# RWKV layers of a six-layer kernel: gate columns on four column groups, R projections in the chunk loop, the bonus term formed earlier, and the two halves of the heads five steps apart

## The chip, the cores and the metric

The kernel runs on one core of one Trainium2 chip. The metric is the time of one execution on the device in microseconds, as the median of several runs. The engines are named as in the profile: PE (TensorE, matrix products), DVE (VectorE), ACT (ScalarE), POOL (GpSimd) and SP (SyncE, which issues DMA transfers). PE runs at one of two levels, 1.2 or 2.4 GHz; the profile gives the granted clock as a share of the full one, so 0.50 is 1.2 GHz.

## What is computed

The model has width 1024, sequence length 256 and 16 heads of 64. It has six layers; two of them (the first, and the fourth) mix over time by RWKV-7, the others by attention, and four have a feed-forward part. The change touches the RWKV mixing only:

```python
r, k, v = rkv[:, :, 0], rkv[:, :, 1], rkv[:, :, 2]      # 1024 x 1024 projections
logw = -softplus(-(w0 + tanh(xw @ w1) @ w2)) - 0.5;  decay = exp(-exp(logw))
a = sigmoid(a0 + (xa @ a1) @ a2)
g = sigmoid(xg @ g1) @ g2                               # the gate, inner width 160
kk = heads(k * k_k), normalised;  k = k * (1 + (a - 1) * k_a)
def step(state, inp):
    sa = einsum('bhvk,bhk->bhv', state, kk_t)
    state = state * w_t - sa[..., None] * (kk_t * a_t) + v_t[..., None] * k_t
    return state, einsum('bhvk,bhk->bhv', state, r_t)
y = group_norm(y) * ln_w + ln_b
y = y + sum(r * k * r_k, axis=-1, keepdims=True) * v    # the bonus term
out = (y * g) @ w_out
```

## The kernel before

**How the step-by-step recurrence is computed.** The 256 steps are two chunks of 128. Within a chunk the recurrence is a triangular linear system for each of the 16 heads, so 32 systems of 128 x 128 unknowns are solved by matrix products. Features lie on the 128 partitions in eight feature chunks c = 0 to 7, two heads in each.

**The stages of one layer.** First come the token mixes, the value projection and the small low-rank products (`lora1` is the first factor of the gate: its inner width of 160 is 128 columns and 32 more, summed over eight slices k of the input). Then the *chunk loop* over c: `kproj` is the key projection, `prep` scales the key vectors by the decay, `amat` forms the products of a system on PE, and `wmat` its right-hand side. `rproj(c)` projects R for a feature chunk, 24 matmuls in split fp32r (lines L117 to L119) plus an elementwise product Rh on DVE; two of the eight are in this loop, six come later.

The *inverse chain* (`inv_diag`) inverts the 32 x 32 diagonal blocks: copies into D by DVE and ACT, a transpose, and 62 dependent DVE operations (L1330 and L1332). While it runs, PE does the remaining R projections and, for every c, `rmat(c)` (products of R with K, L1225) and `rout(c)` (bo, the bonus coefficients, L1237; and the products with V, L1243). rmat's result leaves PSUM by four ACT copies and two POOL masks (L919); the product `prod` on DVE (L1228) has two buffers, freed by bo.

The *merge* (`inv_merge`) puts the inverse together from 32 to 64 to 128: first products L1360, second L1374 and L1376, third L1384, fourth L1387. At four places in it `turn()` calls `gtc`, the gate's second factor, for two feature chunks at a time: a matmul with 128 rows and one with 32 rows for each, into one bank, and a copy to GT (L1266 to L1268).

The *tail* (`rwkv_tail`) is written as a generator with eight steps for each half q of the heads: corrected values (L1425, L1452), state (L1460), outputs (L1435, L1468, L1485), bonus term (L1476, L1478), group norm, transposes (L1498), the gated result z (L1502) and its split og. The two halves A and B run two steps apart; leftover `rout` and `gtc` calls are drawn in by `need`, `need_gate` and `fill`. The output projection (`ohalf`) takes og of each half.

**What sets the order.** The program is written in this order, and a scheduler then decides the order on each engine, with buffers from pools as constraints. Each engine works its own queue strictly in order.

## Time and profile before

| | |
|---|---|
| runs | 1863.23, 1864.0, 1868.2 us (median 1864.0) |
| profiled execution | own time 1852.14 us, span 1850.4 us |
| busy share of the span | PE 95%, DVE 74%, ACT 55%, POOL 2% |
| granted PE clock, mean | 0.952 |
| chain of work that ended last | PE 73%, DVE 14%, DMA 5%, ACT 3%, issue 2% |

The two RWKV layers lie at 0 to 273 us and at about 1085 to 1360 us of the span. A busy share is an average over stages with different limits, and a busy PE at clock 0.50 does half the work; so each stage is read from its own window, with its clock.

### The profile page before, as it was taken

The page shows a single profiled execution, that of the slowest core. Times are in us where ns is not written, and L with a number is a line of the kernel's source. Part 1 is how long each engine was busy: PE and PEld are TensorE (multiplying, and loading weights), DVE is VectorE, ACT ScalarE, POOL GpSimd, SP SyncE. Part 2 cuts the span into 40 slices and gives each one's busy share as a digit, 9 for nine tenths or more (in the row PEclk, how much of TensorE's full clock was granted, in tenths as well). Part 3 has the DMA queues.
Part 4 walks back from the last instruction along what each step waited for, and adds up shares of the span by engine and source line. Part 5 has one row for each costly group of instructions (what it writes and reads, how often), then busy time and mean ns, then how long its engine had stood idle before and what let it go on. Part 6 is the DMA issues. An engine that isn't in the chain of part 4 may idle for free.

```text
span 1850.4 us, 34035 instructions
## 1 busy us (share of the span) xinstructions
PE 1756.0 (95%) x13699; PEld 1575.6 (85%) x13699; DVE 1375.6 (74%) x2710; ACT 1013.8 (55%) x1832; POOL 40.5 (2%) x78
## 2 busy tenths in 40 slices
PE   7998989999999999999999989999899998997998
PEld 5677789999899999877999966787899997885876
DVE  8869489866688876799887568686787656676665
ACT  4755345545576455567645445754265445664664
POOL 0003000000000000000000000021000000000000
PEclk9989789999999999999999999886899999998999
DMA  5211138746427855632685542211065455432540
GB/s 214 103 52 55 59 113 323 259 157 228 168 93 279 288 183 172 237 137 92 239 295 191 182 164 102 73 57 47 35 223 188 170 192 193 160 137 91 181 159 23
DMA packets 52841, 292.19 MB, mean 158 GB/s; under 512 B 6611, under 2 KB 9435, under 8 KB 27980
## 3 DMA queue, kind: packets, MB, share of 16 engines
q1 hardware_dynamic: 48540, 284.64, 43.4%
q10 hardware_dynamic: 4144, 5.39, 0.9%
q8 instruction: 107, 1.75, 0.4%
q14 instruction: 50, 0.41, 0.1%
HBM read 287.90 MB, written 2.10 MB: 157 GB/s over the span
## 4 chain that ended last, share of the span: by engine, by line
PE 73%; DVE 14%; DMA 5%; ACT 3%; issue 2%; DVEq 0%; ACTq 0%
PE mm L117 14%; PE mm L118 14%; PE mm L119 14%; PE mm L222 5%; PE mm L223 5%; PE mm L224 5%; DMA adaw<-ada 4%; DVE wlo L111 3%; DVE junk L678 2%; PE o L511 1%; PE at L475 1%; PE mm L1184 1%; PE at L1165 1%; PE mm L1266 1%; PE mm L1267 1%
## 5 line engine op out<-in xcount | busy, mean ns | idle before, releaser
L111 DVE TENSOR_TENSOR wlo<-wraw,whi 128x1024 fp32r<-128x1024 f32 (+2 forms) x518 | 588.3, 1140 | 229.5 <-ACT whi L110 227.3
L110 ACT CAST whi<-wraw 128x1024 fp32r<-128x1024 f32 (+2 forms) x518 | 504.2, 982 | 296.9 <-PE mm L119 174.3
L222 PE MATMUL mm<-whi,xgh 128*128 128x512 f32 x192 | 80.9, 421 | 8.5 <-ACT xgh L737 8.5
L1549 ACT ACTIVATE sg<-gt 128x256 f32<-128x256 f32 x88 | 36.7, 417 | 90.0 <-DVE gt L1546 89.8
L117 PE MATMUL mm<-mh,whi 128*128 128x256 f32 x256 | 80.9, 316 | 5.0 <-DVE Rh L1097 3.8
L118 PE MATMUL mm<-mh,wlo 128*128 128x256 f32 x256 | 77.9, 304 | 0.0
L119 PE MATMUL mm<-ml,whi 128*128 128x256 f32 x256 | 77.8, 304 | 0.0
L223 PE MATMUL mm<-wlo,xgh 128*128 128x512 f32 x192 | 77.2, 402 | 0.0
L224 PE MATMUL mm<-whi,xgl 128*128 128x512 f32 x192 | 77.0, 402 | 0.0
L678 DVE SCALAR_TENSOR_TENSOR junk<-adaw,cs 128x1024 f32<-128x1024 f32 x48 | 58.6, 1221 | 17.9 <-DMA adaw<-ada 17.7
L1546 DVE TENSOR_TENSOR gt<-mm,rr 128x512 f32<-128x512 f32 x88 | 60.5, 687 | 8.5 <-PE mm L119 5.7
L117 PEld LDWEIGHTS mm<-mh,whi 128*128 128x128 f32 x256 | 55.2, 216 | 9.0 <-DVE Rh L1097 4.0
L118 PE MATMUL mm<-xg0h,wlo 128*128 128x256 f32 x192 | 53.8, 280 | 5.2 <-DVE wlo L111 5.1
L118 PEld LDWEIGHTS mm<-mh,wlo 128*128 128x128 f32 x256 | 55.2, 216 | 1.7 <-issue 1.7
L119 PEld LDWEIGHTS mm<-ml,whi 128*128 128x128 f32 x256 | 54.7, 214 | 1.7 <-issue 1.7
L117 PE MATMUL mm<-xg0h,whi 128*128 128x256 f32 x192 | 54.6, 284 | 0.0
L119 PE MATMUL mm<-xg7l,whi 128*128 128x256 f32 x192 | 53.2, 277 | 0.6 <-DVE xg7l L135 0.6
L222 PEld LDWEIGHTS mm<-whi,xgh 128*128 128x128 f32 x192 | 37.4, 195 | 18.9 <-ACT xgh L737 9.4
L117 PE MATMUL mm<-xg4h,whi 128*128 128x256 f32 x192 | 53.5, 278 | 0.0
L117 PE MATMUL mm<-xg7h,whi 128*128 128x256 f32 x192 | 53.2, 277 | 0.0
L119 PE MATMUL mm<-xg0l,whi 128*128 128x256 f32 x192 | 53.1, 277 | 0.0
L117 PE MATMUL mm<-xg1h,whi 128*128 128x256 f32 x192 | 53.1, 277 | 0.0
(831 smaller groups left out, 6067.1 us busy)
## 6 DMA issues: line engine op xcount, KB each, us to landing
wraw<-ffn_gu SPq DMA_DIRECT2D x88, 1024.0 KB, 6.1
wraw<-ffn_dn SPq DMA_DIRECT2D x64, 704.0 KB, 4.0
adaw<-ada SPq DMA_DIRECT2D x48, 512.0 KB, 5.7
wraw<-hy_qkv SPq DMA_DIRECT2D x24, 1024.0 KB, 4.9
wraw<-rw_k SPq DMA_DIRECT2D x8, 1024.0 KB, 4.9
wraw<-rw_r SPq DMA_DIRECT2D x8, 1024.0 KB, 4.9
wraw<-rw_out SPq DMA_DIRECT2D x8, 1024.0 KB, 4.8
wraw<-sb_qk SPq DMA_DIRECT2D x8, 1024.0 KB, 4.8
```

The lines of the kernel that those rows point to most:

```text
L110: nc.scalar.copy(hi, rw)
L111: nc.vector.tensor_tensor(out=lo, in0=rw, in1=hi.bitcast(F32), op=ALU.subtract)
L117: mm(ps, w[0], x[0], start=first, stop=False, **kw)
L118: mm(ps, w[1], x[0], start=False, stop=False, **kw)
L119: mm(ps, w[0], x[1], start=False, stop=last, **kw)
L222: mm(ps, x[0], w[0], start=first, stop=False)
L223: mm(ps, x[0], w[1], start=False, stop=False)
L224: mm(ps, x[1], w[0], start=False, stop=last)
L475: nc.tensor.matmul(z[e][:, o:o + n], qT[b, hp, t * 128:t * 128 + 128], kT[b, hp, :n], start=True, stop=True)
L678: nc.vector.scalar_tensor_tensor(out=junk, in0=raw, scalar=1.0, in1=self.cs, op0=ALU.mult, op1=ALU.mult, accum_out=self.mod[l][:, j:j + 1])
L1546: nc.vector.tensor_tensor(out=gt, in0=ps.rearrange("p (a b) -> p a b", a=2), in1=r[:, None, :].to_broadcast([128, 2, S]), op=ALU.mult)
L1549: nc.scalar.activation(sg, gt[:, 0], AF.Silu)
```

## The change

The gate's inner 32 columns are computed four times, on the four column groups of PE, so that sg2 lies on all 128 partitions; the gate's second factor then takes four matmuls of 128 rows and four of 32 rows on four row groups into four banks, twice instead of four times, once among the rmat and rout calls and once at the merge's first turn. All eight R projections stand in the chunk loop (RPC says how many at each c). All rmat and rout calls come before the merge. The bonus term bv is formed ahead of the merge, in its own buffer, in place of the eight operations of the tail. The tail has no draw-ins; half A runs alone for five steps, and the projection of its result is laid into half B's steps, two pieces at a time. The weights of the gate's second factor are laid out anew on the host for this, before the launch.

```diff
 BIG = 1e30
 WCH = 2048
-RPC = (3, 6)
-RPN = len(RPC)
-RFR = (0, 0, 2, 2, 2, 2, 3, 3)
-RLAG, RFA, RFB, RFO = 2, 0, 0, 2
+RPC = (0, 0, 1, 1, 1, 1, 2, 2)
+RLAG, RFO = 5, 2
...
-GTP = {}
...
-            sg2 = sp.tile([32, S], F32, name="sg2")
+            sg2 = sp.tile([128, S], F32, name="sg2")
...
-                    for k in range(KT):
-                        t = mix(m, k, "xg_", 8)
+                    for k in range(0, KT, 4):
+                        xt_ = [(k + j, mix(m, k + j, "xg_", 8)) for j in range(4)]
                         for q in range(0, n, 128):
                             p = min(128, n - q)
-                            mm(ps[:p, q // 128 * S:q // 128 * S + S], w[:, o + k * stride + q:o + k * stride + q + p], t,
-                               start=(k == 0 and q == 0), stop=(k == KT - 1), skip_group_check=True)
+                            for k1, t in xt_:
+                                for g in range(0, 128, p):
+                                    mm(ps[g:g + p, q // 128 * S:q // 128 * S + S], w[:, o + k1 * stride + q:o + k1 * stride + q + p], t,
+                                       start=(k1 == 0 and q == 0), stop=(k1 == KT - 1), skip_group_check=True)
                     return ps
...
-                act(sg2, ps[:32, S:], AF.Sigmoid)
+                act(sg2, ps[:, S:], AF.Sigmoid)
...
-                rp = iter(range(RPN))
+                rp = iter(range(KT))
...
                             rnorm(1)
-                    elif c in RPC:
+                    for _ in range(RPC[c]):
                         rproj(rb, next(rp))
                     wmat(c)
                 x2p.close()
                 act(scol, scol, AF.Exp)
+            self.xctx.close()
             with ExitStack() as rde:
                 rd = rde.enter_context(tc.tile_pool(name="rd", bufs=1))
                 TT = [rd.tile([128, 16, 128], F32, name="TT0")]
                 nc.gpsimd.memset(TT[0], 0.0)
                 X = self.inv_diag(rd, AKB)
-                re = rde.enter_context(tc.tile_pool(name="re", bufs=2))
+                rt = rde.enter_context(tc.tile_pool(name="rt", bufs=1, side="right"))
+                GT = rt.tile([128, KT, S], F32, name="GT")
+                TT.append(rt.tile([128, 16, 128], F32, name="TT1"))
+                act(TT[1], self.ones[:, None, :128].to_broadcast([128, 16, 128]), AF.Copy, scale=0.0)
+                g2 = self.wraw.tile([128, WCH], F32, name="wraw")
+                nc.sync.dma_start(g2[:, :1024], self.a["rw_g2a"][l])
+                nc.sync.dma_start(g2[:, 1024:1280], self.a["rw_g2b"][l])
+
+                def gtc(a):
+
+                    pg = [self.psum("at")[:, :S] for _ in range(4)]
+                    for j in range(4):
+                        c = 4 * a + j
+                        mm(pg[j], g2[:, c * 128:128 + c * 128], sg1, start=True, stop=False)
+                    for j in range(4):
+                        b = slice(32 * j, 32 * j + 32)
+                        mm(pg[j], g2[b, 1024 + a * 128:1152 + a * 128], sg2[b], start=False, stop=True)
+                    for j in range(4):
+                        cp(GT[:, 4 * a + j], pg[j])
+                rex = ExitStack()
...
+                re = rex.enter_context(tc.tile_pool(name="re", bufs=2))
                 bo = self.psum("o")
                 ark = [re.tile([128, 4, 128], F32, name=f"ark{j}", bufs=1) for j in range(2)]
                 prods = {}
@@ -1248,62 +1268,39 @@
...
                                               for c in range(KT)), [])
-                for c in range(RPN, KT):
-                    rproj(re, c)
-                    for _ in range(RFR[c]):
-                        rph.pop(0)()
-                self.xctx.close()
-                rt = rde.enter_context(tc.tile_pool(name="rt", bufs=1, side="right"))
-                GT = rt.tile([128, KT, S], F32, name="GT")
-                g2 = self.wraw.tile([128, WCH], F32, name="wraw")
-                nc.sync.dma_start(g2[:, :1024], self.a["rw_g2a"][l])
-                nc.sync.dma_start(g2[:32, 1024:], self.a["rw_g2b"][l])
-
-                def gtc(c0):
-                    pg = self.psum("mm")
-                    for c in (c0, c0 + 1):
-                        o = (c - c0) * S
-                        mm(pg[:, o:o + S], g2[:, c * 128:128 + c * 128], sg1, start=True, stop=False)
-                        mm(pg[:, o:o + S], g2[:32, 1024 + c * 128:1152 + c * 128], sg2, start=False, stop=True)
-                    cp(GT[:, c0:c0 + 2], pg.rearrange("p (a b) -> p a b", a=2))
-                TT.append(rt.tile([128, 16, 128], F32, name="TT1"))
-                act(TT[1], self.ones[:, None, :128].to_broadcast([128, 16, 128]), AF.Copy, scale=0.0)
+                for j, f in enumerate(rph):
...
+                    f()
+                    if j == 8:
+                        gtc(0)
+                rex.close()
+                bv = rde.enter_context(tc.tile_pool(name="rv", bufs=1)).tile([128, 2, 4, 2, 2, 64], F32, name="bv")
+                for q in range(2):
+                    for ch in range(2):
+                        bc = lambda u: u[:, ch, 8 * q:8 * q + 8].rearrange("p (c e) -> p c e", e=2)[:, :, :, None].to_broadcast([128, 4, 2, 64])
+                        tt(out=bv[:, q, :, ch], in0=Vc[:, ch, 512 * q:512 * q + 512].rearrange("p (c e v) -> p c e v", e=2, v=64),
...
                 XNT = self.inv_turn(rd, X)
-                og, gts = [None] * KT, [lambda c=c: gtc(c) for c in range(0, KT, 2)]
-
+                og, gts = [None] * KT, [lambda: gtc(1)]
                 sc = [scr[:, 1024 * q:1024 * q + 1024] for q in range(2)]
-                self.inv_merge([u.rearrange("p a h t -> p (a h) t") for u in AKB], XNT, TT, sc, lambda: gts.pop(0)())
+                self.inv_merge([u.rearrange("p a h t -> p (a h) t") for u in AKB], XNT, TT, sc, lambda: gts and gts.pop()())
...
-                                          sc[q], C, og, lambda: [rph.pop(0)() for _ in range(max(0, len(rph) - 8 * (1 - q)))],
-                                          lambda: [gts.pop(0)() for _ in range(max(0, len(gts) - 2 * (1 - q)))])
+                    return self.rwkv_tail(q, rc, rt, l, Vc, AKB[q], KB, TT[q], csT, Rh, N0, W00, WK1, scol, bv[:, q], GT, sc[q], C, og)
                 add = lambda c, ps: self.new_x(c, x[c], ps)
-                fills = [rph, gts, []]
-
-                def fill(n):
-                    for _ in range(n):
-                        for f in fills:
-                            if f:
-                                f.pop(0)()
-                                break
-                A, B, i = chain(0), chain(1), 0
+                A, B, i, rest = chain(0), chain(1), 0, []
                 while A or B:
-                    if A:
-                        if next(A, 1):
-                            A = None
-                            fills[2] = self.ohalf(self.a["rw_out"][l], 0, og, add)
-                        fill(RFA)
-                    if B and i >= RLAG:
-                        if next(B, 1):
-                            B = None
-                        fill(RFB if A else RFO)
-                    for _ in range(GTP.get(i, 0)):
-                        if gts:
-                            gts.pop(0)()
+                    if A and next(A, 1):
+                        A = None
+                        rest = self.ohalf(self.a["rw_out"][l], 0, og, add)
+                    if B and i >= RLAG and next(B, 1):
+                        B = None
+                    for f in rest[:RFO]:
+                        f()
+                    rest = rest[RFO:]
                     i += 1
-                for f in fills[2] + self.ohalf(self.a["rw_out"][l], 1, og, add):
+                for f in rest + self.ohalf(self.a["rw_out"][l], 1, og, add):
                     f()
             return x
 
@@ -1404,7 +1401,7 @@
...
-        need()
...
                 mm(ps[:, j], TT[:, 8 + 4 * g + j], W1[:, 4 * g + j], start=True, stop=True)
-            (nc.vector.tensor_copy if g else cp)(UP[:, 4 * g:4 * g + 4], ps)
+            cp(UP[:, 4 * g:4 * g + 4], ps)
...
         tt(out=o, in0=y_group(1, lambda j: UP[:, j, :64]), in1=o, op=ALU.add)
         yield
-        bv = TT.rearrange("p h t -> p (h t)")[:, :1024].rearrange("p (c a e v) -> p c a e v", c=4, a=2, e=2)
-        for ch in range(2):
-            bc = lambda u: u[:, ch, hq].rearrange("p (c e) -> p c e", e=2)[:, :, :, None].to_broadcast([128, 4, 2, 64])
-            tt(out=bv[:, :, ch], in0=Vc[:, ch, 512 * q:512 * q + 512].rearrange("p (c e v) -> p c e v", e=2, v=64),
-                                    in1=bc(mu), op=ALU.add)
-            tt(out=bv[:, :, ch], in0=bv[:, :, ch], in1=bc(coef), op=ALU.mult)
         norm(0)
         yield
...
-        need_gate()
...
-    out["rw_g2a"], out["rw_g2b"] = np.ascontiguousarray(f("rw_g2")[:, :128]), np.ascontiguousarray(f("rw_g2")[:, 128:])
+    out["rw_g2a"] = np.ascontiguousarray(f("rw_g2")[:, :128])
+    out["rw_g2b"] = np.ascontiguousarray(f("rw_g2")[:, 128:].reshape(2, 32, 2, 4, 128).transpose(0, 3, 1, 2, 4).reshape(2, 128, 256))
     out["rw_v2"] = np.concatenate([f("rw_v2")[0], f("rw_v0")], 0)
     rk = np.zeros((2, 128, 8, 2), np.float32)
```

PE, between the chunk loop and the merge of the first RWKV layer. Before, a piece of the chain's time, where R projections (mm<-mh,whi and its two partners, 24 matmuls for each) stand between rout (L1237, L1243) and rmat (L1225):

```order
L119 MATMUL mm<-ml,whi 128x256
L1237 MATMUL o<-rkb,prod 128x2 x2
L1243 MATMUL mm<-Vc,ark_1475 128x64 x4
L1225 MATMUL at<-Rh,KB 128x128 x8
L1237 MATMUL o<-rkb,prod 128x2 x2
L1243 MATMUL mm<-Vc,ark_1474 128x64 x4
L117 MATMUL mm<-mh,whi 128x256
L118 MATMUL mm<-mh,wlo 128x256
```

Of the change, from the last W product on (L1245 is rmat, L1257 is bo, L1263 the products of rout):

```order
L1183 MATMUL mm<-Vc,akk_665 128x64 x4
L1245 MATMUL at<-Rh,KB 128x128 x16
L1257 MATMUL o<-rkb,prod 128x2 x6
L1245 MATMUL at<-Rh,KB 128x128 x2
L1263 MATMUL mm<-Vc,ark_1712 128x64 x4
L1245 MATMUL at<-Rh,KB 128x128 x6
L1263 MATMUL mm<-Vc,ark_1713 128x64 x4
L1245 MATMUL at<-Rh,KB 128x128 x8
L1263 MATMUL mm<-Vc,ark_1712 128x64 x4
L1245 MATMUL at<-Rh,KB 128x128 x8
L1257 MATMUL o<-rkb,prod 128x2 x2
```

The projections are gone from between them: rmat and rout follow each other directly, and six bo matmuls (three chunks) stand ahead of the third rmat.

DVE, in the last third of the inverse chain of the same layer (X and tmp are the chain's own tiles). Before:

```order
L1228 TENSOR_TENSOR prod<-Rh,KB 128x256 [waits PE_49]
L1332 TENSOR_TENSOR X__1404<-X__1404,tmp__1407 128x9x23 [waits DVE_49]
L1330 TENSOR_TENSOR tmp__1407<-A__1402,X__1404 128x192 [waits DVE_49]
L1332 TENSOR_TENSOR X__1404<-X__1404,tmp__1407 128x8x24 [waits DVE_49]
L1330 TENSOR_TENSOR tmp__1407<-A__1402,X__1404 128x175 [waits DVE_49]
L1332 TENSOR_TENSOR X__1404<-X__1404,tmp__1407 128x7x25 [waits DVE_49]
L1330 TENSOR_TENSOR tmp__1407<-A__1402,X__1404 128x156 [waits DVE_49]
L111 TENSOR_TENSOR wlo<-wraw,whi 128x1024 [waits DMAHW1_49,Activation_49]
L1332 TENSOR_TENSOR X__1404<-X__1404,tmp__1407 128x6x26 [waits DVE_49]
L1097 TENSOR_TENSOR Rh<-mm,E1r 128x256 [waits PE_49]
```

Of the change, the same place:

```order
L1327 TENSOR_TENSOR tmp__1636<-A__1631,X__1633 128x207 [waits DVE_49]
L1329 TENSOR_TENSOR X__1633<-X__1633,tmp__1636 128x9x23 [waits DVE_49]
L1280 TENSOR_TENSOR bv<-Vc,mu 128x4x128 [waits PE_49,Pool_49]
L1327 TENSOR_TENSOR tmp__1636<-A__1631,X__1633 128x192 [waits DVE_49]
L1282 TENSOR_TENSOR bv<-bv,coef 128x4x128 [waits DVE_49]
L1329 TENSOR_TENSOR X__1633<-X__1633,tmp__1636 128x8x24 [waits DVE_49]
L1280 TENSOR_TENSOR bv<-Vc,mu 128x4x128
L1327 TENSOR_TENSOR tmp__1636<-A__1631,X__1633 128x175 [waits DVE_49]
L1282 TENSOR_TENSOR bv<-bv,coef 128x4x128 [waits DVE_49]
L1329 TENSOR_TENSOR X__1633<-X__1633,tmp__1636 128x7x25 [waits DVE_49]
```

The products of prod, the weight halves (wlo) and Rh have left this place, and the bonus term's operations (L1280, L1282) stand between those of the chain; the first of them waits for PE and POOL.

PE, at the start of the merge (sg and wraw are the gate's inner values and its weights; XN and AKB the merge's first product). Before:

```order
L1225 MATMUL at<-Rh,KB 128x128 x8
L1237 MATMUL o<-rkb,prod 128x2 x4
L1360 MATMUL mm<-XN__1883,AKB_625 32x32 x32
L1360 MATMUL mm<-XN__1883,AKB_626 32x32 x32
L1266 MATMUL mm<-sg_112,wraw 128x256
L1267 MATMUL mm<-sg_113,wraw 128x256
L1266 MATMUL mm<-sg_112,wraw 128x256
L1267 MATMUL mm<-sg_113,wraw 128x256
L1374 MATMUL mm<-M_1887,XT__1885 32x32
L1376 MATMUL at<-XT__1885,M_1887 32x32 x2
```

Of the change:

```order
L1257 MATMUL o<-rkb,prod 128x2 x2
L1226 MATMUL at<-sg_112,wraw 128x256 x2
L1263 MATMUL mm<-Vc,ark_1713 128x64 x4
L1226 MATMUL at<-sg_112,wraw 128x256 x2
L1229 MATMUL at<-sg_113,wraw 128x256 x4
L1357 MATMUL mm<-XN__1953,AKB_649 32x32 x32
L1357 MATMUL mm<-XN__1953,AKB_650 32x32 x32
L1371 MATMUL mm<-M_1957,XT__1955 32x32 x16
L1373 MATMUL at<-XT__1955,M_1957 32x32 x32
```

The gate's second product now stands around the last rout, ahead of the merge's first product, and none stands inside the merge.

## Rows read from the trace of the kernel before

**Rows 1.** Windows: span, engines' busy us (instructions), granted PE clock, DMA share, GB/s.
```profile
97.00:138.40 41.40, 38.04 (x280) 32.69 (x278) 29.85 (x76) 21.36 (x63) 1.03 (x2) 0.84 0.09 31
...
144.90:183.50 38.60, 30.80 (x278) 28.85 (x276) 37.02 (x81) 19.47 (x53) 13.12 (x16) 0.92 0.16 56
183.50:216.70 33.20, 33.15 (x480) 23.65 (x480) 10.35 (x15) 14.55 (x21) 0.00 (x0) 0.57 0.15 46
216.70:247.40 30.70, 25.08 (x284) 23.43 (x283) 24.33 (x55) 7.68 (x20) 0.00 (x0) 0.92 0.10 39
247.40:273.30 25.90, 25.90 (x201) 25.80 (x200) 21.69 (x49) 14.94 (x28) 0.00 (x0) 0.90 0.43 164
...
1269.20:1302.20 33.00, 32.98 (x480) 23.50 (x480) 10.37 (x15) 14.53 (x21) 0.00 (x0) 0.59 0.14 45
```

**Rows 2.** Timeline of PE in an R projection: start, us, instruction.
```profile
143.40 0.28 PE L117 MATMUL mm<-mh,whi 128*128 128x256 f32 x1
...
145.75 0.28 PE L119 MATMUL mm<-ml,whi 128*128 128x256 f32 x1
```

**Rows 3.** Timeline of ACT; in brackets idle time before, and its releaser.
```profile
138.87 4.50 ACT L1319 COPY D__1393<-AKB 32x512 f32<-32x512 f32 x4
...
144.34 0.64 ACT L1231 COPY ark<-at 128x256 f32<-128x256 f32 x2
...
175.33 1.91 ACT L1270 ACTIVATE TT<-ones 128x2048 f32<-128x2048 f32 x1 [2.15 <-PE mm L119]
...
200.84 0.59 ACT L1268 COPY GT<-mm 128x512 f32<-128x512 f32 x1 [4.04 <-PE mm L1267]
```

**Rows 4.** Timeline of DVE, chain and half B's last og.
```profile
143.40 1.25 DVE L1322 STREAM_TRANSPOSE A__1402<-D__1393 128x1024 f32<-128x1024 f32 x1
...
144.98 1.21 DVE L111 TENSOR_TENSOR wlo<-wraw,whi 128x1024 fp32r<-128x1024 f32 x1
...
181.55 1.91 DVE L1338 STREAM_TRANSPOSE XN__1883<-X__1404 128x1024 f32<-128x1024 f32 x1
...
258.13 0.43 DVE L1504 TENSOR_TENSOR og<-z,og 128x256 fp32r<-128x256 f32 x1
```

**Rows 5.** Timeline of PE in the chunk loop, half clock and full.
```profile
123.62 1.22 PE L1165 MATMUL at<-aT,KB 64*128 64x128 f32 x8 [1.93 <-DVE KB L1155]
...
127.88 1.23 PE L1165 MATMUL at<-aT,KB 64*128 64x128 f32 x8
...
134.12 1.00 PE L1184 MATMUL mm<-Vc,akk 128*128 128x64 f32 x8
135.06 1.16 PE L1165 MATMUL at<-aT,KB 64*128 64x128 f32 x16
```

**Rows 6.** Windows in the merge, columns as in rows 1.
```profile
204.00:208.00 4.00, 4.00 (x11) 1.93 (x10) 0.00 (x0) 0.58 (x1) 0.00 (x0) 0.50 0.00 0
...
212.00:216.00 4.00, 4.00 (x40) 2.61 (x37) 0.80 (x2) 1.17 (x2) 0.00 (x0) 1.00 0.41 98
```

**Rows 7.** Timeline of PE, merge and tail.
```profile
205.48 1.22 PE L1267 MATMUL mm<-sg,wraw 32*128 32x256 f32 x2
...
214.70 2.08 PE L1387 MATMUL at<-TT,aT 64*64 64x64 f32 x32
...
225.08 2.00 PE L1243 MATMUL mm<-Vc,ark 128*128 128x64 f32 x16
```

**Rows 8.** Groups by line and shape: line, operation, shapes, count, busy us, mean ns.
```profile
L1008 PE MATMUL mm<-xm,G 128*128 128x256 f32 x16 | 5.5, 424 | 0.0
L1008 PE MATMUL mm<-xm,G 128*32 128x256 f32 x16 | 5.0, 391 | 0.0
...
L1452 PE MATMUL at<-WK,TT 128*128 128x128 f32 x32 | 4.2, 280 | 0.0
...
L1468 PE MATMUL at<-KB,AKB 128*64 128x128 f32 x32 | 2.2, 279 | 0.0
...
L1476 DVE TENSOR_TENSOR TT<-Vc,mu 128x512 f32<-128x512 f32 x4 | 2.7, 688 | 2.0 <-PE mm L1425 2.0
```

More of the change, by code (lines that the diff above doesn't have):

```diff
@@ L1269, in rwkv @@
-                TT.append(rt.tile([128, 16, 128], F32, name="TT1"))
-                act(TT[1], self.ones[:, None, :128].to_broadcast([128, 16, 128]), AF.Copy, scale=0.0)
+                for j, f in enumerate(rph):
[8 more added lines that the diff above has]
+                        tt(out=bv[:, q, :, ch], in0=Vc[:, ch, 512 * q:512 * q + 512].rearrange("p (c e v) -> p c e v", e=2, v=64),
+                           in1=bc(mu), op=ALU.add)
+                        tt(out=bv[:, q, :, ch], in0=bv[:, q, :, ch], in1=bc(coef), op=ALU.mult)
@@ L1278, in chain @@
                 def chain(q):
-                    return self.rwkv_tail(q, rc, rt, l, mu, Vc, AKB[q], KB, TT[q], csT, Rh, N0, W00, WK1, scol, coef, GT,
-                                          sc[q], C, og, lambda: [rph.pop(0)() for _ in range(max(0, len(rph) - 8 * (1 - q)))],
-                                          lambda: [gts.pop(0)() for _ in range(max(0, len(gts) - 2 * (1 - q)))])
+                    return self.rwkv_tail(q, rc, rt, l, Vc, AKB[q], KB, TT[q], csT, Rh, N0, W00, WK1, scol, bv[:, q], GT, sc[q], C, og)
@@ L1405, in inv_merge, with rwkv_tail @@
                 turn()
-    def rwkv_tail(self, q, rc, rt, l, mu, Vc, AKB, KB, TT, csT, Rh, N0, W00, WK1, scol, coef, GT, scr, C, og, need, need_gate):
+    def rwkv_tail(self, q, rc, rt, l, Vc, AKB, KB, TT, csT, Rh, N0, W00, WK1, scol, bv, GT, scr, C, og):
         nc = self.nc
```

## The prediction

> **What bounds the kernel now.** I read the busy shares of the page first, to see that no engine is full everywhere, then the timeline of one RWKV layer engine by engine, then windows cut at its stage borders, and last the granted clock in those windows, because the same work of TensorE (PE) costs twice as much at the lower of its two levels (0.5 of 2.4 GHz, that is 1.2 GHz). The change touches only the two RWKV layers; they read alike (the merge takes 33 us and a clock of 0.57 to 0.59 in both), so I work out one and count it twice [rows 1].
>
> The reader is to see five stages with different limits. In the chunk loop (97 to 138.4) PE is busy 38 of 41 us, part of it at half clock. In the inverse chain (144.9 to 183.5) VectorE (DVE) is busy 37 of 38.6 us: it runs 62 dependent small operations, one stream, and everything else that it is given lies in the middle of them. In the merge (183.5 to 216.7) PE is busy throughout, but at a clock of 0.57. The tail of the heads (216.7 to 247.4) shares its time between PE and DVE, and the output projection up to the next layer's first matmul (247.4 to 273.3) is PE again [rows 1].
>
> **The change, part by part.**
>
> *The R projections.* One costs 24 matmuls; 20 steps take 2.35 us at full clock, so 2.82 us each [rows 2]. Six move from the chain's time into the chunk loop, 16.9 us. The loop's 38.0 us of busy PE at a clock of 0.84 would be about 31.4 us at full clock. (Half of the time is lost where the clock is 0.5, so the share at half is 0.32, 13.2 us, worth 6.6 us.) I take full clock, since the projections fill the idle time after which the clock fell, and take off 2 us of such work that the loop already holds: 31.4 + 16.9 - 2 = 46.3 us, a loop that ends near 143.3 instead of 138.4. ScalarE (ACT) then copies the diagonal blocks, 4.5 us [rows 3], DVE transposes, 1.25 us [rows 4]; ACT first zeroes TT1, 1.91 us [rows 3], which waits for the last projection and partly lies beside PE's last W work. The chain starts at about 149.5 instead of 144.9: **+4.6**. Bounds: +3 if the loop gains more, +6.5 if the zeroing lies wholly in the path.
>
> *The chain itself.* It loses four weight halves of 1.13 us (the step from 144.98 to the next operation) and five Rh of about 0.33, and gains eight operations of the bonus term, 0.69 each [rows 4, 8]: 36.7 - 4.5 - 1.7 + 5.4 = 35.9 us if nothing waits. But two kinds of wait are in it by the order of DVE: prod(5) to prod(7), each for bo(c-2) on PE, since prod has two buffers; and the first bonus operation, for rout(7) and GpSimd's last mask, since it takes their space. DVE works in order, so the chain stands still with them.
>
> When is PE there? After the loop, PE does rmat(0) and rmat(1), and then waits for the four banks, which ACT empties only behind its copies: 143.3 + 2 to 149.5 or so it has nothing. Before, an idle time of 1.93 us sufficed: from 123.62 it ran at half clock, rmat-like work of 8 instructions in 1.2 us where 16 took 1.16 at full [rows 5]. So I take rmat at 2.4 us and rout at 2.0 from 150 on. bo(3) stands behind three rmat and three rout: 150.3 + 13.2 = 163.5. DVE reaches prod(5) at about 158: a wait of 5.5 us. Then comes the gate's first product, eight instructions of 128 rows, two of which take 1.15 to 1.22 us at half clock, and the small ones together, about 5.8 us, to 171 [rows 7].
>
> *Does the clock come back there?* In the merge of before, PE was busy from 183.5 to 208 and stayed at 0.50; at 212 to 216 it had 1.00 [rows 6]. What stood between was the gate's product and then two strands of 64-row matmuls side by side. The new product puts four matmuls of 128 rows back to back and four of 32 rows side by side, with no half-empty ones between, so I take it that the clock is full after it, from 171 on. Against it: the gate's product of 204.33 alone did not suffice. The Trainium skill ("TensorE: Matmul & The Clock Gate", Part 1, "What's actually happening") says that the half rate is the default and that sustained activity releases it. By that rule rmat and rout, which keep PE busy, would soon run at full clock and the waits of this part would go; the trace disagrees for work of this shape, with 24 us of busy PE at 0.50 [rows 1, 6]. It is the second rival below.
>
> With full clock from 171 (rmat 1.1 us, rout 1.0 [rows 5]), bo(4) is done at 172.5; DVE, at prod(6) by 170, waits 2.5 us. prod(7) does not wait. PE goes on at 2.4 us per chunk, above ACT's (four copies, two of which take 0.64 us, and one of csT [rows 3]), and ends rout(7) near 180.2; DVE, at the bonus term by 179.4, waits 0.8 us. The waits are 8.8 us. GpSimd's masks, which by my estimate slow DVE for some 5 us in all, then fall partly into them, which gives back about 3. The chain ends at 149.5 + 35.9 + 8.8 - 3 = 191.2 instead of 181.55: 9.7 later, of which **+5.1** beyond its start. The transpose after it, 1.91 us beside a mask [rows 4], takes 1.2 when GpSimd is done: **-0.7**.
>
> *The merge.* Four gate products leave it. Each held 4.6 us at half clock (8 instructions at 0.575) and the last 2.5, of which ACT's copies of M and TT would hide some in the first: ACT waited 4.04 us for a gate product [rows 3, 7]. The first gives 3.9, the second 4, the third 3.9, the last 1.8, and the work in the place of the last parts runs at half clock longer, 2 us: 33.2 becomes about 21.5, **-11.7**. Bounds: -10 with ACT as the limit, -14 if PE has full clock there.
>
> *The tail.* Rout of two chunks goes (2.0 us [rows 7]), the bonus term goes from DVE (5.5 us of the 24 it was busy [rows 1, 8]) and one UP copy per half from DVE to ACT. PE's own work is about 22.5 us at full clock. The clock is half at its start, since the merge now ends with fewer paired matmuls; I add 3 us for that: 25.5 instead of 30.7, **-5.2**. Bounds: -6.7 (full clock), and +14 (half clock throughout, 2 x 22.5 = 45).
>
> *Output projection.* Half B was ready 10.7 us after half A's projection began [rows 4], and PE never waited. With five steps between them, half A's 96 matmuls (11.3 us) end before DVE has done B's second norm, four z and four og, with weight halves and new_x between: some 15 us. I take **+3.4** (bounds 0 and +5).
>
> *The gate's 32 columns.* Sixteen instructions of 32 columns become 64, on four column groups. If these run side by side, nothing changes. Two groups do: L1468 (64 columns) has 32 instructions in 2.2 us, L1452 (128) 32 in 4.2 [rows 8]. I take **0**; one after another they would cost 48 x 0.31 = 15 us per layer (16 took 5.0 [rows 8]). The Trainium skill ("TensorEngine Tiling (Array Packing)", "Key Properties") has tiles work independently, but says that a change of the tiling mode drains the engine; here the mode changes twice per four k, which no row of before prices, and by which the sum would be a little higher.
>
> The sum for a layer is 4.6 + 5.1 - 0.7 - 11.7 - 5.2 + 3.4 = -4.5 us; for both -9.0. From the profiled execution's own 1852.1 us that gives 1843.1; the median of the runs lies 11.9 us above it, so **1855 us** in the runs.
>
> **The rivals.**
>
> 1. *The low clock stays after the gate's product (slower).* What speaks for it: the row of 204 to 208 at 0.50 [rows 6]. Then bo(4), bo(5) and rout(7) come at 174, 179 and 190, the chain ends near 200, 18.5 us later than before, and the layer is at 18.5 - 0.7 - 11.7 - 3.2 + 3.4 = +6.3, so 1877; with half clock through the tail too (+14.3 instead of -3.2) at +23.8, so 1912. It decides if the rmat behind the gate's first product still takes 2.4 us. Chance 0.20.
>
> 2. *The clock hardly falls, or comes back within rmat (faster).* No waits in the chain, it ends at 185.4, +3.9; with -0.7, a merge at -12 to -14, a tail at -6.7 and +3.4 a layer gains 12 to 14 us: 1838. For it: in 144.9 to 183.5 the clock was 0.92 [rows 1]. Against: PE had dense projections there, which are gone. Chance 0.17.
>
> 3. *No change.* The later chain start (+6.5), the gap in the projection (+5) and a merge at -10.7 eat the rest: -4.5 + 1.9 + 1.6 + 1.0 = 0, 1864. Chance 0.16.
>
> 4. *The column groups run one after another.* +30 on the forecast, 1885. Against it the 64-column rows [rows 8]. Chance 0.07.
>
> **How the numbers follow.** The case of the sum has 0.40. Two executions of this kernel differ by 0.3% (5.6 us), so that is the bound between change and none: 1858.4 and 1869.6. The sum's own case, 1846 to 1865, gives 0.27 to faster, 0.11 to same and 0.02 to slower; rival 2 gives 0.17 to faster; rival 3 gives 0.03, 0.09 and 0.04; rivals 1 and 4 give 0.27 to slower. Faster 0.47, same 0.20, slower 0.33. The range goes from just below rival 2 (1837) to just beyond rival 4 (1890); what lies outside is the faster end of rival 2 and the half-clock tail of rival 1. The likeliest case alone is 1846 to 1865.
>
> **What would show it.** Right: PE idle for 4 us or more before the third rmat, a clock near 0.5 from 150 to 170 and full after the gate's first product; DVE waiting in the chain at a prod for PE, 5 us; XN's transpose some 10 us later in the layer than before; a merge of 21 to 22 us; a tail near 25 us; an idle time of PE between the halves of the projection. Wrong, if rout(7) ends with the chain still far from the bonus term (the waits are gone), if the tail runs at 0.5 throughout, or if L1008's 64 small instructions take longer than 5 us.

## The result, and the profile after

The change makes the kernel 0.8% faster: a median of 1847.6 us over 4 runs (1844.7 to 1851.3) against 1863.6 (1861.1 to 1868.2), a ratio of 0.9917 with an interval of 0.9893 to 0.9940. The forecast was 1855; the time came out 16 us lower than before, not 9. The profiled execution took 1851.25 us, with a span of 1849.5 at a mean clock of 0.961, which seems to say that nothing was gained over the profiled execution of before (span 1850.4). The layers and the feed-forward parts must therefore be read apart.

The windows of the changed kernel at the borders of the same stages (the columns are those of [rows 1]) answer to the rows shown there: the chunk loop, the time up to the chain, the chain, the merge, the tail, the output projection, and last the merge of the second RWKV layer:

```profile
97.00:143.00 46.00, 46.00 (x427) 42.90 (x425) 34.73 (x80) 28.01 (x70) 3.47 (x4) 1.00 0.24 84
143.00:149.80 6.80, 2.00 (x10) 1.83 (x11) 4.46 (x8) 6.73 (x13) 1.59 (x4) 0.67 0.00 0
149.80:190.20 40.40, 31.46 (x212) 27.08 (x210) 32.67 (x77) 14.74 (x46) 10.58 (x15) 0.71 0.15 53
192.10:212.30 20.20, 20.18 (x448) 20.07 (x448) 9.16 (x14) 11.92 (x16) 0.00 (x0) 0.55 0.07 15
212.30:235.20 22.90, 22.73 (x266) 21.27 (x264) 14.26 (x33) 6.75 (x17) 0.00 (x0) 1.00 0.05 13
235.20:262.40 27.20, 24.33 (x200) 23.31 (x200) 24.76 (x60) 14.61 (x29) 0.00 (x0) 1.00 0.41 155
1280.40:1300.90 20.50, 20.45 (x449) 20.32 (x449) 9.18 (x14) 11.92 (x16) 0.00 (x0) 0.55 0.05 15
```

The chunk loop is now full PE work at full clock. PE then stands still for 4.8 of 6.8 us, first for `prod` on DVE and then for ACT's copies. The chain has a clock of 0.71 where it had 0.92 [rows 1]. The merge is 13 us shorter at the same low clock, and the tail 7.8 us shorter. From the loop's first `amat` (at 87.8 us, before at 88.5) to the first matmul of the stage after the output projection, the first RWKV layer takes 174.7 us instead of 184.7, the second 174.2 instead of 183.6: 19.4 us in all.

Shorter windows of the changed kernel show the clock through chain and merge; the last two have the times of [rows 6], though the tail begins at 212.3 here:

```profile
152.00:156.00 4.00, 4.00 (x22) 3.66 (x21) 3.06 (x7) 2.71 (x6) 1.06 (x2) 0.50 0.01 2
...
164.00:168.00 4.00, 4.00 (x13) 3.17 (x12) 3.72 (x9) 0.45 (x2) 0.43 (x1) 0.50 0.00 0
...
172.00:176.00 4.00, 4.00 (x48) 3.75 (x48) 3.86 (x7) 2.35 (x8) 2.83 (x4) 1.00 0.00 0
204.00:208.00 4.00, 4.00 (x43) 4.00 (x43) 0.00 (x0) 1.40 (x3) 0.00 (x0) 0.50 0.00 0
212.00:216.00 4.00, 4.00 (x40) 3.93 (x39) 0.86 (x2) 1.17 (x2) 0.00 (x0) 1.00 0.26 73
```

PE's timeline shows what it did there: rmat (L1245) at half clock after an idle time, bo(3) (L1257), the gate's first product (L1226, L1229), then rmat at full clock, 16 instructions in 1.43 us where they took 2.08 at 160. The last row is the longest idle time of PE in the output projection:

```profile
149.24 1.22 PE L1245 MATMUL at<-Rh,KB 64*128 64x128 f32 x4 [2.17 <-ACT KB L1251]
...
162.10 1.01 PE L1257 MATMUL o<-rkb,prod 128*128 128x2 f32 x4
...
164.71 3.73 PE L1226 MATMUL at<-sg,wraw 128*128 128x256 f32 x8
168.37 1.07 PE L1229 MATMUL at<-sg,wraw 32*128 32x256 f32 x8
169.88 1.43 PE L1245 MATMUL at<-Rh,KB 64*128 64x128 f32 x16 [0.45 <-ACT GT L1231]
...
249.18 0.38 PE L114 MATMUL mm<-og,whi 128*128 128x256 f32 x1 [1.05 <-ACT og L1492]
```

DVE's timeline shows the new waits: one of 0.80 us for ACT before the one weight half that is left in the chain, prod(5) and prod(6) for PE, 3.80 and 1.44 us, and none at the bonus term (L1280). XN's transpose is 8.6 us later in the kernel than in [rows 4]:

```profile
153.85 1.23 DVE L108 TENSOR_TENSOR wlo<-wraw,whi 128x1024 fp32r<-128x1024 f32 x1 [0.80 <-ACT whi L107]
...
163.15 0.79 DVE L1248 TENSOR_TENSOR prod<-Rh,KB 128x256 f32<-128x256 f32 x1 [3.80 <-PE o L1257]
...
170.02 0.42 DVE L1327 TENSOR_TENSOR tmp__1636<-A__1631,X__1633 128x256 f32<-128x256 f32 x1
171.89 0.43 DVE L1248 TENSOR_TENSOR prod<-Rh,KB 128x256 f32<-128x256 f32 x1 [1.44 <-PE o L1257]
172.23 0.85 DVE L1329 TENSOR_TENSOR X__1633<-X__1633,tmp__1636 128x256 f32<-128x256 f32 x1
...
181.16 0.69 DVE L1280 TENSOR_TENSOR bv<-Vc,mu 128x512 f32<-128x512 f32 x1
...
190.16 1.90 DVE L1335 STREAM_TRANSPOSE XN__1953<-X__1633 128x1024 f32<-128x1024 f32 x1
```

The spans of the two first profiles differ by 0.9 us only, so 18.5 us were lost elsewhere: in the feed-forward parts, whose code the change leaves alone. Two windows of the kernel before, in dense 128x256 work at full clock, each with PE busy throughout:

```profile
380.00:420.00 40.00, 40.00 (x356) 40.00 (x355) 25.83 (x38) 19.84 (x34) 0.00 (x0) 1.00 0.49 164
...
1000.00:1040.00 40.00, 40.00 (x355) 40.00 (x354) 26.00 (x38) 20.12 (x31) 0.00 (x0) 1.00 0.48 162
```

The same windows of the changed kernel hold 342 matmuls instead of 355:

```profile
380.00:420.00 40.00, 40.00 (x342) 40.00 (x341) 24.36 (x36) 19.43 (x31) 0.00 (x0) 1.00 0.50 164
...
1000.00:1040.00 40.00, 40.00 (x342) 40.00 (x341) 24.51 (x34) 18.73 (x29) 0.00 (x0) 1.00 0.44 147
```

That is one matmul per 117 ns instead of 113. Both spacings occur in both kernels: a second execution of the kernel before has 342 in its window of 380 to 420, and a second one of the changed kernel has 355, as these rows show in this order:

```profile
380.00:420.00 40.00, 40.00 (x342) 40.00 (x341) 25.41 (x37) 19.38 (x31) 0.00 (x0) 1.00 0.43 146
...
380.00:420.00 40.00, 40.00 (x355) 40.00 (x354) 24.82 (x38) 20.27 (x33) 0.00 (x0) 1.00 0.53 182
```

So the two first profiles hide a gain that the medians show. Whether the change makes the wider spacing more frequent was not tested.

### The profile page after: what moved, and what is told of

Same layout as the page of the kernel before. It is cut to its first block, busy times and chain, and to the rows that moved or that the text cites. A ratio compares the mean times of both kernels' runs of the same rounds, so it can differ in the third digit from the quotient of the medians.

```text
span 1849.5 us, 34252 instructions
## 1 busy us (share of the span) xinstructions
PE 1748.0 (95%) x13795; PEld 1589.3 (86%) x13795; DVE 1369.1 (74%) x2706; ACT 1017.2 (55%) x1844; POOL 35.5 (2%) x78
## 5 line engine op out<-in xcount | busy, mean ns | idle before, releaser
L114 PE MATMUL mm<-mh,whi 128*128 128x256 f32 x256 | 73.9, 289 | 1.7 <-ACT sg L1070 1.7
L116 PE MATMUL mm<-ml,whi 128*128 128x256 f32 x256 | 72.6, 284 | 0.0
L115 PE MATMUL mm<-mh,wlo 128*128 128x256 f32 x256 | 72.6, 283 | 0.0
L114 PE MATMUL mm<-xg5h,whi 128*128 128x256 f32 x192 | 53.7, 280 | 0.0
L116 PE MATMUL mm<-xg4l,whi 128*128 128x256 f32 x192 | 53.7, 280 | 0.0
L115 PE MATMUL mm<-xg5h,wlo 128*128 128x256 f32 x192 | 53.7, 280 | 0.0
L115 PE MATMUL mm<-xg4h,wlo 128*128 128x256 f32 x192 | 53.7, 280 | 0.0
L114 PE MATMUL mm<-xg6h,whi 128*128 128x256 f32 x192 | 53.7, 280 | 0.0
L115 PE MATMUL mm<-xg6h,wlo 128*128 128x256 f32 x192 | 53.7, 280 | 0.0
```

Of the source, the lines that this page charges most:

```text
L114: mm(ps, w[0], x[0], start=first, stop=False, **kw)
L115: mm(ps, w[1], x[0], start=False, stop=False, **kw)
L116: mm(ps, w[0], x[1], start=False, stop=last, **kw)
```

## Experiments

My reading after the result was this: the price of the change is a later start of the chain and PE at half clock in it, and this stays small because the gate's first product, put among rmat and rout, brings the clock back; the gain is the gate's work that leaves the merge, and the tail. The rival reading: the clock comes back in the chain anyway, and the product's place does not matter. Later the question was which part of the tail's gain is whose, and whether filling PE's hole pays.

**The kernels again.** The kernel before in one execution, and the changed kernel timed twice more.

> The kernel before again, nothing changed, for a second profile. In the first two profiles the dense matmuls of the feed-forward parts follow each other at 113 ns in the kernel before and at 118 ns in three of the four feed-forward parts of the changed kernel, although the change does not touch them; that is some 19 us in favour of the profile before. Theory A, it varies from execution to execution: here some feed-forward parts are at 118 ns and the RWKV layers are within 0.5 us of the first profile, stage by stage. Theory B, it belongs to the program: 113 ns in all of them again.

> The changed kernel again. Time 1844 to 1852 us, 0.989 to 0.994 of the kernel before. The RWKV layers as in its first profile: chain of the inverse ends at 190.2, tail begins at 212.3, projection at 235.2 (each within 0.5 us). By theory A (above) the spacing in the feed-forward parts may be 113 or 118 ns, by theory B it is 118 ns in the same three.

> The changed kernel a third time, in more rounds, for the ratio and a third profile: 0.985 to 0.994 of the kernel before. In its two profiles the merge and the tail took 20.2 to 20.4 and 22.9 us in three of four layers and 22.0 and 25.7 us in the fourth, where the clock came back some 3 us later. Theory, this varies from execution to execution: here each layer has one of the two pairs again.

Before: 1866.6 us. Its first RWKV layer took 190.8 us, 6.0 more than in the first profile, since the clock came back late: merge 37.2 and tail 36.0 us instead of 33.2 and 30.7. Its second layer took 184.0. The changed kernel: 1842.8 us, ratio 0.9899 (0.9832 to 0.9967), and 1848.0, ratio 0.9915 (0.9888 to 0.9942). In both, the first layer has a merge and tail of 20.2 and 22.9 us, the second of 22.0 and 25.7. The moment at which the clock returns in the merge is not fixed by the program.

**The gate's first product back in the merge.**

```
-                    if j == 8:
-                        gtc(0)
-                og, gts = [None] * KT, [lambda: gtc(1)]
+                og, gts = [None] * KT, [lambda: gtc(1), lambda: gtc(0)]
```

> The changed kernel with the gate's first product moved from the rmat and rout calls to the second turn of the merge. Theory 1, that product brings the clock back: without it the clock is 0.50 from 150 to 181 or so, rout of chunk 7 ends 2 to 4 us later, the chain ends 1 to 4 us later, and the merge is 4 to 6 us longer for the product in it: 5 to 9 us per layer, 10 to 18 us slower than the changed kernel. Theory 2, the clock comes back by itself from the length of busy time: it is full again by 171, the chain ends some 4 us earlier for the product that has gone, and the merge takes it back: within 4 us of the changed kernel.

Measured 1864.5 us, ratio 1.0009 (0.9974 to 1.0044), beside 1842.8 for the changed kernel in the same measurement: the whole gain is gone. Windows of the chain, of rmat and rout within it, and of the merge:

```profile
149.90:196.50 46.60, 36.46 (x195) 32.40 (x194) 32.44 (x77) 13.47 (x42) 10.13 (x15) 0.54 0.07 24
152.00:184.00 32.00, 32.00 (x176) 29.50 (x176) 18.52 (x39) 11.57 (x35) 8.15 (x12) 0.50 0.10 34
198.40:225.40 27.00, 26.96 (x465) 23.87 (x465) 9.15 (x14) 13.23 (x20) 0.00 (x0) 0.53 0.15 50
```

DVE's timeline, its wait at the first operation of the bonus term:

```profile
183.61 0.69 DVE L1278 TENSOR_TENSOR bv<-Vc,mu 128x512 f32<-128x512 f32 x1 [5.37 <-PE mm L1263]
```

PE is busy for all of the 32 us, with rmat and rout and at their end with the other product, and has a clock of 0.50 throughout, so the rival reading falls. That other product, which the scheduler lays around the last rout as in the change (179.8 to 186.4 us here), is again followed by a higher clock (0.74 from 184 to 188), too late for the chain. The chain becomes 6.2 us longer, with waits for PE of 3.81, 1.10, 1.41 and 5.37 us, and the merge 6.7, since a product now lies in it. So low a clock to the end of rout is what rival 1 feared, though there the product stays in the chain.

**The hole after the loop filled** with ten idle matmuls behind rmat(1), whose results nothing reads.

```
+                    if j == 1:
+                        for _ in range(10):
+                            mm(bo[:, 256:512], self.ident, sg1, start=True, stop=True)
```

> The changed kernel with ten idle matmuls of 128 x 256 (results never read) on PE after the second rmat, in the time in which PE waits for ACT. Theory 1, the half clock after that idle time makes the waits of the inverse chain: the granted clock stays at 1.00 from 143 to 182, bo of chunk 3 is done near 158 instead of 163, the waits for prod (3.8 and 1.4 us) go, the chain ends 4 to 5 us earlier in each RWKV layer, the kernel is 7 to 10 us faster than the changed one. Theory 2, the waits come from prod's two buffers and from ACT's and GpSimd's part of each chunk, whatever the clock: the clock is full, but DVE still waits 3 us or more at prod, and the time is the changed kernel's within 3 us.

Measured 1841.2 us, ratio 0.9898 (0.9826 to 0.9969), beside 1842.8 for the changed kernel in the same measurement. Windows of chain, merge and tail:

```profile
149.10:184.10 35.00, 25.39 (x220) 21.35 (x220) 33.35 (x78) 14.37 (x47) 10.63 (x16) 0.93 0.18 61
186.00:208.00 22.00, 21.98 (x448) 21.81 (x448) 9.14 (x14) 11.93 (x16) 0.00 (x0) 0.50 0.06 18
208.00:236.50 28.50, 28.29 (x266) 26.73 (x265) 14.46 (x34) 6.91 (x17) 0.00 (x0) 0.79 0.03 8
```

In the first layer the waits at prod are gone and the chain is 5.4 us shorter. But the merge keeps its clock of 0.50 to the end, 1.8 us longer, and the tail begins at half clock, 5.6 us longer: what the chain gave is given back. In the second layer, where a wait of 1.6 us at prod is left, the chain gained 3.6 us, and merge and tail lost 4.3 against the first profile of the change, with the same late return (22.0 and 25.7 us) as a repeat of the change without the fill. The late return is thus not the fill's alone.

**The bonus term held back into the merge.** Its eight operations are issued behind XT's transpose.

```
-                for q in range(2):
...
+                with tc.issue_after(self.xtr):
+                    for q in range(2):
...
-        nc.vector.transpose(XT.rearrange("p a b -> p (a b)"), X.rearrange("p a b -> p (a b)"))
+        self.xtr = nc.vector.transpose(XT.rearrange("p a b -> p (a b)"), X.rearrange("p a b -> p (a b)")).ins
```

> The changed kernel with the bonus term's eight operations held back on DVE until the transposes after the inverse chain, so that they lie in the merge, where DVE was idle for more than half of the time. Theory 1, each operation costs its full length in the chain: the chain is 5 us shorter (35 instead of 40.4 us), the merge at most 2 us longer, the layer 3 to 5 us shorter, the kernel 6 to 10 us faster than the changed one. Theory 2, what the chain gains is given back by PE's clock, which comes back in the merge or the tail at a moment that does not move with the chain: merge 22 us and tail 26 to 28 us as with the filled idle time, the layer within 1 us of the changed kernel.

Measured 1826.2 us, ratio 0.9822 (0.9749 to 0.9896). Windows of the chain and the merge:

```profile
149.60:186.00 36.40, 31.34 (x211) 27.06 (x210) 28.54 (x68) 14.72 (x46) 10.59 (x15) 0.73 0.17 59
188.00:208.30 20.30, 20.30 (x448) 20.19 (x448) 12.33 (x20) 11.95 (x16) 0.00 (x0) 0.55 0.05 15
```

The chain loses 4 us and the merge, where DVE is busy 9 of 20 us, takes the work at no cost: 3.7 and 4.2 us per layer. These 7.9 us are what the edit is shown to give. The median lies 17 to 22 us below those of the change, but in this profiled execution all four feed-forward windows that were read hold 355 or 356 matmuls, in the change's first profile one of four; no run separates the rest from that.

**Halves two steps apart, as before** (`RLAG, RFO = 2, 2`).

> The changed kernel with the two halves of the heads two steps apart instead of five. Theory 1, the distance shortens the tail and costs a gap in the projection: from the tail's start to the projection 26 to 29 us instead of 22.9, the projection 1 to 2 us shorter (25.5 instead of 27.1), 3 to 5 us per layer, 5 to 10 us slower. Theory 2, the shorter tail comes from the work that left it and from the full clock, not from the distance: each within 1 us, the time that of the changed kernel.

Measured 1852.4 us, ratio 0.9948 (0.9909 to 0.9987). The next experiment, timed together with it and with the five steps of the change, took 1848.9 us; the times alone do not tell the two apart, the stages do. Windows at the end of the first layer's tail, then tail and projection of the second layer:

```profile
239.00:243.00 4.00, 0.78 (x10) 0.47 (x8) 3.96 (x12) 1.36 (x5) 0.00 (x0) 0.82 0.00 0
243.00:247.00 4.00, 1.59 (x7) 1.22 (x8) 4.00 (x13) 1.02 (x4) 0.00 (x0) 0.50 0.00 0
...
1295.20:1324.10 28.90, 23.27 (x267) 21.62 (x267) 18.60 (x45) 7.99 (x20) 0.00 (x0) 0.93 0.06 10
1324.10:1348.90 24.80, 24.80 (x201) 24.68 (x199) 21.59 (x49) 14.91 (x28) 0.00 (x0) 0.94 0.45 170
```

At the end of the tail DVE works nearly alone, on the norms of both halves, PE idles and its clock falls. The tail before ended so too:

```profile
240.00:244.00 4.00, 0.62 (x3) 0.39 (x4) 3.96 (x14) 1.35 (x5) 0.00 (x0) 0.81 0.00 0
244.00:248.00 4.00, 1.75 (x9) 1.39 (x9) 4.00 (x13) 1.30 (x5) 0.00 (x0) 0.50 0.00 2
```

With five steps between them, half B's norms lie under half A's projection. In the second layer, where the clock came back as in the change, the tail is 28.9 instead of 22.9 and the projection 24.8 instead of 25.9: the five steps are worth 4.9 us net per layer.

**The gate's columns alternating in shape for each k.**

```
-                    for k in range(0, KT, 4):
-                        xt_ = [(k + j, mix(m, k + j, "xg_", 8)) for j in range(4)]
+                    for k in range(KT):
+                        xt_ = [(k, mix(m, k, "xg_", 8))]
```

> The changed kernel with the first gate product in the old order: for each of the eight slices k the 128-column matmul and then the 32-column ones on four column groups, instead of four slices at a time. In the changed kernel 80 instructions took 7.5 us where the 32 of before took 9.4. Theory 1, each change between 128-column and 32-column tiles costs some 0.1 us on PE, and the grouping by four saved it: the product takes 9 to 10.5 us here. Theory 2, the four groups side by side made it shorter: 7.5 us here too. The whole changes by less than can be measured.

Measured 1848.9 us, ratio 0.9928 (0.9893 to 0.9963), not to be told from the change. Groups by line and shape, of the changed kernel and then of this one (each product appears as two instructions):

```profile
L1007 PE MATMUL mm<-xm,G 128*128 128x256 f32 x16 | 3.9, 385 | 0.0
L1007 PE MATMUL mm<-xm,G 128*32 128x256 f32 x64 | 3.9, 382 | 0.0
```

```profile
L1007 PE MATMUL mm<-xm,G 128*128 128x256 f32 x16 | 5.5, 424 | 0.0
L1007 PE MATMUL mm<-xm,G 128*32 128x256 f32 x64 | 5.1, 391 | 0.0
```

With as many changes of shape as before, 64 small instructions take 5.1 us where 16 took 5.0 [rows 8]: the four column groups run side by side. The stretch of this product lasts 9.55 us here, 9.39 before and 7.54 in the change. The Trainium skill ("TensorEngine Tiling (Array Packing)", "Key Properties") has a change of the tiling mode drain the engine; the trace fits that: for each slice k the shape changes to 32 columns and back, for four slices at a time only once so, and 16 such changes made 4 saved 2.0 us, some 0.17 us each. I had applied the rule with the wrong sign, since the kernel before changed shape more often.

**The projections alone in the loop** (the kernel before with six instead of two there, `RPC = (2, 3, 4, 5, 6, 7)`, and the calls that went with them at the end).

> The kernel before with one part of the change alone: six of the eight R projections in the chunk loop (one for each c from 2 to 7), two left after it; gate products, bonus term and tail as before. Theory 1, the move by itself is no gain: the chain starts 3 to 4 us later, loses some 4 us of weight halves and Rh, and the lower clock after the loop makes waits in it; up to the merge the layer is 0 to 6 us longer, and the merge is 33 us as before; time 1862 to 1876. Theory 2, the move is where the gain of the change is from: the layer is 3 us or more shorter up to the merge, and the kernel 6 us or more faster than before.

Measured 1855.2 us, ratio 0.9971 (0.9932 to 1.0010). Windows of loop and chain:

```profile
97.00:136.90 39.90, 39.90 (x361) 36.87 (x358) 33.65 (x82) 27.36 (x75) 1.04 (x2) 1.00 0.20 71
144.60:178.00 33.40, 25.40 (x178) 23.42 (x176) 30.01 (x72) 13.07 (x35) 9.37 (x14) 0.63 0.16 60
```

From the loop's first `amat` to the merge the first layer takes 91.8 us instead of 95.0, the second 92.5 instead of 94.8, and the first merge its old 33.2. The second layer of the profiled execution got its clock back late (merge 37.1, tail 35.8). A gain of 2 to 3 us per layer is what the run suggests; the interval of the times does not show it. It comes near theory 2 in the first layer and falls short of it in the second. What bears on the change: with four more projections in the loop the chain starts 56.5 us after the first `amat`, before after 56.4, in the change after 62.1. Four of the six cost the loop no time, so the later start comes with the last two or with what else the change lays before the chain. The changed kernel with only four of them moved was not tried.

**Both: bonus in the merge and the hole filled.** The two edits above together; in a second version twelve more idle matmuls stand behind the last rout.

> The changed kernel with the bonus term held back into the merge and with the ten idle matmuls after the second rmat. Theory 1, both gains of the chain add up: the chain 31 to 32 us (36.3 with the bonus term alone, 35 to 37 with the fill alone, 40.4 without), the layer 3 to 5 us shorter than with the bonus term alone, 6 to 10 us less in all. Theory 2, the earlier end of the chain is given back by the clock, which comes back later in the merge or the tail as with the fill alone (22.0 and 25.7 to 28.5 us): the layer within 2 us of that with the bonus term alone.

> As the kernel with both edits, with twelve more idle matmuls of 128 x 256 in PE's idle time before the merge (half of the gate's second product then lands inside the merge). Theory 1, dense work up to the merge keeps the clock through its start: the merge is 17 to 19 us instead of 20.3 to 22, and the tail 22.9. Theory 2, the small matmuls of the merge let the clock fall anyway within some 4 us, and it comes back at the merge's end or in the tail: merge and tail together 43 us or more, as without the extra matmuls.

Measured 1829.4 us, ratio 0.9837 (0.9795 to 0.9879), and 1828.6, ratio 0.9847 (0.9803 to 0.9891). Windows of the first version: the chain of its second layer, merge and tail of its first.

```profile
1228.00:1259.00 31.00, 25.39 (x220) 21.34 (x220) 29.14 (x69) 13.94 (x47) 10.61 (x15) 0.94 0.09 35
185.60:207.60 22.00, 22.00 (x449) 21.81 (x449) 12.80 (x20) 11.95 (x16) 0.00 (x0) 0.51 0.12 34
207.60:233.20 25.60, 25.40 (x265) 23.96 (x264) 15.56 (x36) 6.78 (x17) 0.00 (x0) 0.89 0.03 8
```

The chain is the shortest of all, 31 to 33 us. Merge and tail give it back: 47.6 us together instead of 43.2 with the bonus moved alone. The second version buys the tail's clock (22.9 us) with a longer merge (24.5 to 25.0). Its idle matmuls (L1279) stand ahead of the merge, and they push part of the gate's second product (L1226) into it, which in this layer begins at 188.16:

```profile
182.83 5.40 PE L1279 MATMUL o<-sg,ident 128*128 128x256 f32 x24
...
191.89 2.08 PE L1226 MATMUL at<-sg,wraw 128*128 128x256 f32 x4
```

Against the bonus moved alone, the fill gains nothing that the times show, and the two layers together take 341 to 342 us with it and without. The best kernel is that with the bonus term in the merge, with the fill or without: the first version's interval (0.9795 to 0.9879) lies below that of the change beside it (0.9888 to 0.9942).

## Why the prediction was right, and where its sizes were off

The direction, the mechanism and the range held; the gain was twice the forecast's per layer. The 1847.6 us lie at the lower edge of the likeliest case (1846 to 1865), and one repeat, 1842.8, lies below it. Step by step, first layer and second where they differ:

- *Start of the chain*, forecast +4.6: measured 4.95 later in the kernel (149.82 instead of 144.87). The loop became 46.0 us at full clock (forecast 46.3), so the clock that the projections restore did pay for part of them; the run with four of them moved says that it paid for those four in full.
- *The chain*, forecast +5.1 beyond its start: +3.7 and +4.7. Clock 0.50 from 152 on, full behind the gate's product, bo(3) at 163.1 (forecast 163.5): all seen. The waits for PE were 3.80, 1.44 and 0 us instead of 5.5, 2.5 and 0.8, since DVE came later to each. On the way to prod(5) it had lost 0.80 us to the wait for ACT, which the sum does not have, and 1.9 us to operations that took longer than others of their size. The trace ties these to GpSimd: 22 of the 124 chain operations of both layers took over 0.12 us more than the shortest of their size, and each of them lies beside a mask in time (the 0.85 us at 172.23 in the rows above beside two masks at 171.98 to 173.58, the 0.42 us at 170.02 beside none); no run takes the masks away. In all they cost 4.9 us per layer, before 5.7, so the estimate of some 5 us was good, but what fell into the waits was 0.8 and not 3. Waits of 6.0 instead of 8.8 and a smaller give-back nearly cancel; that the term comes within 1.4 us is in part luck. That the gate's product decides over the clock is shown by the run that moved it.
- *Transpose*, forecast -0.7: 0. It took 1.90 us as before [rows 4].
- *Merge*, forecast -11.7: -13.0 and -12.6 in the first profile, -11.1 in the layers in which the clock returned late. The term lies in that spread.
- *Tail and projection*: here a term was mis-sized. Forecast -5.2 and +3.4, together -1.8; measured -7.8 and +1.3 (+0.8), together -6.5 and -7.0. The tail lies even below the bound of -6.7, with PE busy for 22.7 of its 22.9 us. I credited it with the work taken out of it, and entered the five steps between the halves as a cost alone. The run with two steps shows the opposite: the work taken out gives 1.8 us of the tail (30.7 to 28.9), the five steps 6.0 of the tail for 1.1 of the projection. What I overlooked stood in the trace: at 240 to 248 PE was nearly idle, waiting for DVE's end of both halves. Of the 5.6 us by which the first layer's gain exceeded its forecast, this is 4.7. The 3 us added for half clock at the tail's start were not spent in the first profile (clock 1.00), and were in others (25.7 us).
- *Column groups*, forecast 0: side by side, as taken. The stretch became 1.9 us shorter for the fewer changes of shape, but the loop's first `amat` comes 40.8 us after the product's start, before 40.9: nearly nothing of it reaches the loop.

Rival 1 did not come. The run with the product in the merge, where the clock stayed low, costs 12.9 and 13.2 us per layer more than the change, but about half of that is the longer merge, in which a product lies; rival 1 as it was stated, with the product in the chain, was in no run. Rival 3, no change, did not come either. Rival 2's chain, without a wait for PE, exists in single layers of the filled kernels; what it left out is that merge and tail give such a gain back. Rival 4 is refuted.

## What to carry to other kernels

Where two engines hand a stage's end to each other, look for the last few microseconds in which only one works: letting one half run ahead, so that this end lies under the next stage's matmuls, was worth more here (4.9 us net) than taking work out of the stage (1.8). Work that has slack should go where its engine is idle, not where it is nearest: eight operations in a chain that bounds cost 4 us, and in the merge nothing. And one product can decide over the clock of a long stretch: here the gate's, some 5 us in the middle of rmat and rout, was followed by full clock, and without it the clock was 0.50 to the end of rout; where such a product stands is part of the schedule.

## What the runs showed of the hardware

Dense 128x256 matmuls at a granted clock of 1.00 ran at one per 113 ns in some stretches and one per 117 in others (355 or 342 in 40 us), and differently in different executions of one kernel; between the two first profiles this makes most of the 18.5 us that lie outside the RWKV layers. No run here shows why. A busy PE is no sign of a full clock: with the gate's product moved away, PE was busy for all of 152 to 184 us, mostly on rmat and rout, at a granted clock of 0.50. DVE's operations in the chain took up to twice as long where a mask of GpSimd lay beside them (0.85 us instead of 0.42 for 128x256, at 172.23 and 170.02). The clock's return in the merge differs between executions by 2 to 4 us of the merge and 3 to 5 of the tail; a gain of under 1% has therefore to be read from the stages, and from several executions.
